# One Hymba layer on one core: the input stages as three queues, stepped behind every contraction tile of the projections

## The chip, the core and the metric

The kernel runs on one core of one Trainium2 chip. The metric is the device time of one execution in microseconds. Three runs of the kernel before took 1739.31 to 1742.88 us, with a median of 1740.18 us. Of the core's engines the text speaks of PE (TensorE, the matmuls), DVE (VectorE), ACT (ScalarE), POOL (GpSimd) and SP (SyncE, which issues the DMAs). Each engine executes its instructions in the order in which the program lists them, and waits where an operand isn't there yet.

## The reference

One layer for 1024 prompt rows and 64 sample rows of width 1024: an adaLN-modulated norm, one input projection whose columns go to 8 RWKV-7 heads and to 8 heads of forgetting attention (FoX), one output projection, and a SwiGLU network. All in fp32.

```python
mod = jax.nn.silu(c) @ w_ada + b_ada
h = _rms_norm(x, norm1_g) * (1 + sc1[:, None]) + sh1[:, None]
proj = h @ w_in
p_rwkv, p_fox = proj[..., :RWKV_COLS], proj[..., RWKV_COLS:]
z = (p_rwkv + (prev - p_rwkv) * shift_mu)            # prev: the row before
r, k, v, dw, da, dg = jnp.split(z, list(RWKV_SPLITS), axis=-1)
decay, a, g = f(tanh(dw) @ w_decay_up), sigmoid(da @ w_aaa_up), sigmoid(dg) @ w_gate_up
...
def step(s, inp):                                    # _rwkv_scan, over the rows
    r_t, w_t, k_t, v_t, kk_t, a_t = inp
    sa = jnp.einsum('bhvk,bhk->bhv', s, -kk_t)
    s = (s * w_t[:, :, None, :] + sa[..., None] * (kk_t * a_t)[:, :, None, :]
         + v_t[..., None] * k_t[:, :, None, :])
    return s, jnp.einsum('bhvk,bhk->bhv', s, r_t)
...
y_fox = _fox_mixer(q, k_all, v_all, lc_all, past)    # softmax(q k + decay bias) v, causal
mix = jnp.concatenate([y_rwkv, y_fox], axis=-1) @ w_out
x = x + gt1[:, None] * mix
ffn = (jax.nn.silu(h2 @ w_ffn_gate) * (h2 @ w_ffn_up)) @ w_ffn_down
```

## The kernel before

The 1088 columns (rows of the reference, laid along the free dimension) are worked in two halves: half 0 has 512 prompt columns, half 1 has 512 prompt and 64 sample columns in two chunks of 288. The normed h of a half lies in SBUF as a high and a low part (`hhi`, `hlo`). `proj` (L298) takes one block of 128 weight columns, splits it in a high and a low part, and multiplies it in `mm3` (L290): three matmuls `pmm` (L294, L295, L296) for each of the 8 tiles of the contraction. They write to a PSUM bank with the tag "mm". PSUM has the further tags "ra", "rb", "ch" and "fx" for the small work. Between the projections stands the small work of the two kinds of heads:

- The RWKV heads go in four pairs j = 0 to 3 per half. `proj_z` computes and shifts the three z of a pair. `rwkv_d` gives decay and a. `rwkv_a` prepares the pair: sums over heads (`pbs`, L375), the products `pA` of each chunk of 64 columns (L464), masked into `At` on DVE (L466), then the triangular systems: `dm` and `mb` through DRAM (L476, L479), 15 steps on DVE with `tb` and `wb` (L488, L490), a transposed copy `mb<-wb` (L491), and the results `dw`, `du` to DRAM (L497).
- `rwkv_b` reads them back as `gt` and `inv` (L513, L514) and merges the 16x16 blocks to 64x64 by small matmuls of 32x32: `pg`, `pw`, `pu`, `pgt` (L523) and `pu` again (L549), each of which needs a copy of the one before. Then come transposes (`pkbt`, `pvt`) and the chain: for each chunk pR (L597), a copy, pSA (L610), a copy, pS (L613), a product on DVE (L617), and pR of the next chunk. Half 0 has 8 chunks for each pair, half 1 has 9.
- `rwkv_n` norms and gates the output y, and writes it to DRAM as `yscr` (L646).
- For FoX, `fox_qk`, `fox_v`, `logf` and `cache_kv` norm, split and store queries, keys, values and the forget sums. `ada_mm` and `ada_fin` (L190, L198) compute the 24 adaLN tiles that later stages need, one with each projection, on a "mm" bank: matmuls with the weights `wada`, a copy `mrow` on ACT, a transpose. `x_stat1` gathers the norm of half 1.

`phase` runs these in the order of a string per half. Capital letters start work, small ones finish it: Z the three z of a pair, D, A, B and N the routines above, Q, K, V the projections of FoX and q, k their norms, C the cache, L `logf`, S `x_stat1`, P early loads of the attention, T and U the last chain of half 0 inside half 1.

```python
ORDER = ("Z0 D0 A0 L B0 D1 Z1 Q0 N0 A1 C0 Z2 q0 D2 V0 O A2 K0 k0 B1 K1 Z3 Q1 q1 V1 N1 D3 A3 V2 C1 S k1 Q2 Q3 B2 q2 N2 K2 k2 V3 K3 k3 C2 C3 q3",
         "T3 Z0 D0 A0 L Z1 K0 D1 U3 B0 A1 D2 Z2 Q0 N0 k0 A2 q0 D3 Q1 B1 K1 q1 Z3 A3 k1 V2 N1 V1 B2 V0 Q2 q2 K3 N2 Q3 q3 P B3 K2 k3 k2 V3")
```

Whole routines stand in the program one after the other. What each engine then executes in which order is settled by a list scheduler at build time: it has the dependences and, as its priority, the place in the program. So a B that stands ahead of a projection is laid between that projection's matmuls as its links come ready. Behind the last projection follow the attention (`psc` scores, `ppt` transposes, `pav` value products), which fills the last pair's chain too, the output projection `po`, and the FFN (`pd` and `pf`), from 778.7 us to the end at 1734.2.

Of the kernel before, what the change touches and what calls it, by code (L numbers as in the profile page):

```python
# [7 lines left out]
F32 = mybir.dt.float32  # L8
# [8 lines left out]
P = 128  # L17
D = 1024
KT = D // P
SP = 1024  # L20
SS = 64
# [13 lines left out]
ORDER = ("Z0 D0 A0 L B0 D1 Z1 Q0 N0 A1 C0 Z2 q0 D2 V0 O A2 K0 k0 B1 K1 Z3 Q1 q1 V1 N1 D3 A3 V2 C1 S k1 Q2 Q3 B2 q2 N2 K2 k2 V3 K3 k3 C2 C3 q3",  # L35
         "T3 Z0 D0 A0 L Z1 K0 D1 U3 B0 A1 D2 Z2 Q0 N0 k0 A2 q0 D3 Q1 B1 K1 q1 Z3 A3 k1 V2 N1 V1 B2 V0 Q2 q2 K3 N2 Q3 q3 P B3 K2 k3 k2 V3")
# [28 lines left out]
class K:  # L65
# [128 lines left out]

    def ada_fin(self, part):
# [36 lines left out]
    def x_stat1(self):  # L232

        nc = self.nc
        acc = self.zpool.tile([P, 576], F32, tag="z", name="xacc")
# [12 lines left out]
        return self.x_rms(Half(1), acc)  # L248

    def x_rms(self, hf, rs):  # L250
        nc, n = self.nc, hf.n
        for off, m in hf.chunks:
            ps = self.ps([P, 512], tag="mm", name="pxs")
# [55 lines left out]

    def proj_z(self, hf, zi):  # L310
# [8 lines left out]
        z = self.zpool.tile([P, 576], F32, tag="z", name="z")  # L319
# [68 lines left out]
    def rwkv_d(self, hf, j, zl):  # L388
# [6 lines left out]
        for off, m in hf.chunks:  # L395
# [8 lines left out]
            for x, (dst, base) in enumerate(((sw, V_W0), (a, V_A0))):  # L404
                nc.vector.tensor_scalar(dst[:, off:off + m], ps[x][:, 0:m], col(base), -43.0, op0=ALU.add, op1=ALU.max)
        self.sigm(sw[:, 0:n], 1.0)
        self.sigm(a[:, 0:n], 1.0)
        cum = self.slot(name="cum", tag="sa")
# [6 lines left out]
        return a, cum  # L415

    def rwkv_a(self, hf, j, z, d):

        nc, vc, O = self.nc, self.vc, self.O
# [4 lines left out]
        zk, zr, zv, sq = z  # L424
        a, ip = d
        pp = self.pp
# [5 lines left out]
            rn[:, off:off + m], ps, 1e-24, None, op0=ALU.max), "ra")  # L432
        nc.scalar.activation(rn[:, 0:n], rn[:, 0:n], AF.Ln, scale=1.0 / 64)
# [4 lines left out]
        kb = self.rpool.tile([P, 9, P], F32, tag="kb", name="kb")  # L438
        nc.vector.tensor_tensor(rk[:, 0:nch, 0:64], ch(kk), pp[:, 0:nch, 0:64], op=ALU.mult)
        nc.vector.tensor_tensor(rk[:, 0:nch, 64:128], ch(zr), pp[:, 0:nch, 1:65], op=ALU.mult)  # L440
        nc.vector.tensor_tensor(kk[:, 0:n], kk[:, 0:n], a[:, 0:n], op=ALU.mult)
        for h in range(2):
            hp = slice(64 * h, 64 * h + 64)
            nc.vector.tensor_tensor(kb[hp, 0:nch, hp], ch(kk)[hp], ch(ip)[hp], op=ALU.mult)
        nc.vector.tensor_scalar(a[:, 0:n], a[:, 0:n], col(V_KA), self.oka[:, j:j + 1], op0=ALU.mult, op1=ALU.add)
        nc.vector.tensor_tensor(zk[:, 0:n], zk[:, 0:n], a[:, 0:n], op=ALU.mult)
        for h in range(2):
            hp, oc = slice(64 * h, 64 * h + 64), slice(64 - 64 * h, 128 - 64 * h)
            nc.vector.tensor_tensor(kb[hp, 0:nch, oc], ch(zk)[hp], ch(ip)[hp], op=ALU.mult)

        nc.vector.scalar_tensor_tensor(zr[:, 0:n], zr[:, 0:n], col(V_RK), zk[:, 0:n], op0=ALU.mult, op1=ALU.mult)
        bon = self.slot(name="bon", tag="bon")
# [1249 lines left out]
```

## Time and profile before

| | |
|---|---|
| median of 3 runs | 1740.18 us (1739.31 to 1742.88) |
| the profiled execution's own time | 1735.94 us, span 1734.2 us |
| mean granted clock of PE | 0.981 |
| first pmm to last pmm (projections and input stages) | 34.8 to 692.3 us |
| from there to the first matmul of the output projection | 692.3 to 778.7 us |
| in the span: PE, DVE, ACT, POOL busy | 1663.8, 1126.6, 729.1, 180.8 us |

In a row of the time line stand start, length (us), engine, line, operation, what is written from what, the shape, and in brackets how long the engine was idle ahead of it and what ended that. In a row of the waits stand engine, operation and line, what was waited for, and the us in total, how often, and the longest. The length of a matmul is modelled and covers that of its neighbours; the rate is read from one start to the next. A wait of an engine that nobody waits for costs nothing.

### The profile page before, as it was taken

The page shows a single profiled execution, that of the slowest core. Times are in us where ns is not written, and L with a number is a line of the kernel's source. Part 1 is how long each engine was busy: PE and PEld are TensorE (multiplying, and loading weights), DVE is VectorE, ACT ScalarE, POOL GpSimd, SP SyncE. Part 2 cuts the span into 40 slices and gives each one's busy share as a digit, 9 for nine tenths or more (in the row PEclk, how much of TensorE's full clock was granted, in tenths as well). Part 3 has the DMA queues.
Part 4 walks back from the last instruction along what each step waited for, and adds up shares of the span by engine and source line. Part 5 has one row for each costly group of instructions (what it writes and reads, how often), then busy time and mean ns, then how long its engine had stood idle before and what let it go on. Part 6 is the DMA issues. An engine that isn't in the chain of part 4 may idle for free.

```text
span 1734.2 us, 33257 instructions
## 1 busy us (share of the span) xinstructions
PE 1663.8 (96%) x12893; PEld 1447.9 (83%) x12893; DVE 1126.6 (65%) x2574; ACT 729.1 (42%) x1532; POOL 180.8 (10%) x412
## 2 busy tenths in 40 slices
PE   5999999999999999889999989999999999999999
PEld 3676766688888888766888889999999999999998
DVE  6676676757686753876877686666666655555545
ACT  4534454553454445765776453333233223211210
POOL 2102121131221212300210000000000000000000
PEclk9999999999899999989999999999999999999999
DMA  8535457632233344566553333222222224433213
GB/s 314 149 95 137 142 140 207 175 93 56 55 76 75 95 121 136 157 194 177 151 177 136 127 115 101 75 75 75 76 75 82 78 87 143 161 98 98 95 37 122
DMA packets 133581, 207.09 MB, mean 119 GB/s; under 512 B 62126, under 2 KB 70350, under 8 KB 133422
## 3 DMA queue, kind: packets, MB, share of 16 engines
q1 hardware_dynamic: 133422, 204.95, 39.3%
q8 instruction: 102, 1.67, 0.4%
q14 instruction: 57, 0.47, 0.1%
HBM read 157.65 MB, written 47.25 MB: 118 GB/s over the span
## 4 chain that ended last, share of the span: by engine, by line
PE 82%; DVE 7%; ACT 7%; DMA 2%; issue 2%; SPq 1%; POOL 0%; DVEq 0%; ACTq 0%; POOLq 0%
PE pd L1264 15%; PE pfc L1153 8%; PE pfe L1153 8%; PE pfa L1153 7%; PE pmm L294 5%; PE pmm L296 5%; PE pmm L295 5%; PE pfb L1153 4%; PE pav L962 2%; PE pbs L375 2%; PE pA L464 2%; PE ppt L940 2%; PE po L294 1%; PE po L295 1%; PE po L296 1%
## 5 line engine op out<-in xcount | busy, mean ns | idle before, releaser
L294 PE MATMUL pmm<-hhi,whi 128*128 128x288 f32 (+1 forms) x624 | 220.7, 354 | 0.7 <-ACT pb L317 0.7
L295 PE MATMUL pmm<-hlo,whi 128*128 128x288 f32 (+1 forms) x624 | 218.2, 350 | 0.0
L296 PE MATMUL pmm<-hhi,wlo 128*128 128x288 f32 (+1 forms) x624 | 218.0, 349 | 0.0
L212 ACT CAST whi<-wraw 128x1024 fp32r<-128x1024 f32 (+2 forms) x116 | 99.3, 856 | 214.4 <-PE pd L1264 167.0
L1264 PE MATMUL pd<-ah,wlo 128*128 128x512 f32 (+1 forms) x528 | 173.5, 329 | 0.0
L1264 PE MATMUL pd<-al,whi 128*128 128x512 f32 (+1 forms) x528 | 173.2, 328 | 0.0
L1264 PE MATMUL pd<-ah,whi 128*128 128x512 f32 (+1 forms) x528 | 173.0, 328 | 0.0
L1268 DVE SCALAR_TENSOR_TENSOR x1t<-pd,mod,x1t 128x512 f32<-128x512 f32 x192 | 91.4, 498 | 110.6 <-PE pd L1264 110.0
L294 PEld LDWEIGHTS pmm<-hhi,whi 128*128 128x128 f32 x624 | 120.3, 193 | 13.5 <-ACT pb L317 2.0
L296 PEld LDWEIGHTS pmm<-hhi,wlo 128*128 128x128 f32 x624 | 120.3, 193 | 10.9 <-issue 1.7
L295 PEld LDWEIGHTS pmm<-hlo,whi 128*128 128x128 f32 x624 | 120.4, 193 | 9.6 <-issue 0.7
L216 DVE TENSOR_TENSOR wlo<-wraw,whi 128x1024 fp32r<-128x1024 f32 (+2 forms) x108 | 103.8, 961 | 26.0 <-ACT whi L212 25.6
L1153 PE MATMUL pfc<-hh,hS 128*128 128x256 f32 (+1 forms) x352 | 102.0, 290 | 4.4 <-ACT hh L1055 4.4
L1264 PEld LDWEIGHTS pd<-al,whi 128*128 128x128 f32 x528 | 99.4, 188 | 7.7
L1264 PEld LDWEIGHTS pd<-ah,whi 128*128 128x128 f32 x528 | 99.3, 188 | 7.7
L1264 PEld LDWEIGHTS pd<-ah,wlo 128*128 128x128 f32 x528 | 99.2, 188 | 7.4
L1153 PE MATMUL pfc<-hl,hS 128*128 128x256 f32 (+1 forms) x352 | 102.3, 290 | 0.0
L1153 PE MATMUL pfc<-hh,lS 128*128 128x256 f32 (+1 forms) x352 | 102.0, 290 | 0.0
L1153 PE MATMUL pfa<-hl,whi 128*128 128x256 f32 (+1 forms) x352 | 101.8, 289 | 0.0
L1153 PE MATMUL pfa<-hh,whi 128*128 128x256 f32 (+1 forms) x352 | 101.7, 289 | 0.0
L1153 PE MATMUL pfa<-hh,wlo 128*128 128x256 f32 (+1 forms) x352 | 101.4, 289 | 0.0
L604 POOL TENSOR_SCALAR sd<-sv,pc 64x64 f32<-64x64 f32 x136 | 72.0, 529 | 172.9 <-DVE sv L617 156.6
(360 smaller groups left out, 4402.0 us busy)
## 6 DMA issues: line engine op xcount, KB each, us to landing
wraw<-in_w_in_dram SPq DMA_DIRECT2D x52, 512.0 KB
wada<-in_w_ada_dram SPq DMA_DIRECT2D x48, 512.0 KB
as<-actscr SPq DMA_DIRECT2D x22, 544.0 KB
wraw<-in_w_gate_dram SPq DMA_DIRECT2D x22, 512.0 KB
wraw<-in_w_up_dram SPq DMA_DIRECT2D x22, 512.0 KB
wraw<-in_w_down_dram SPq DMA_DIRECT2D x40, 256.0 KB
wraw<-in_w_out_dram SPq DMA_DIRECT2D x16, 512.0 KB
actscr<-sg SPq DMA_DIRECT2D x22, 288.0 KB
```

The source lines that it names most:

```text
L212: nc.scalar.copy(hi, src)
L216: eng.tensor_tensor(lo, src, hi.bitcast(F32), op=ALU.subtract)
L294: nc.tensor.matmul(ps[0:M, 0:n], whi[:, k, 0:M], xhi[:, k, off:off + n], start=(k == 0), stop=False)
L295: nc.tensor.matmul(ps[0:M, 0:n], whi[:, k, 0:M], xlo[:, k, off:off + n], start=False, stop=False)
L296: nc.tensor.matmul(ps[0:M, 0:n], wlo[:, k, 0:M], xhi[:, k, off:off + n], start=False, stop=(k == kt - 1))
L375: nc.tensor.matmul(ps[:, 0:n], w, x[:, off:off + n], start=True, stop=True)
L464: nc.tensor.matmul(pa[h][:, i], kb[hp, c + i], rk[hp, c + i], start=True, stop=True)
L604: nc.gpsimd.tensor_scalar(sd[hsl[h]], sv[hsl[h], c, h], pc[hsl[h], c], None, op0=ALU.mult)
L940: nc.tensor.transpose(pt[0:rows, b - b0, t * P:t * P + qn], p[0:qn, pc:pc + rows], self.ident[0:qn, 0:qn])
L1153: nc.tensor.matmul(ps, l[:, k], r[:, s, k], start=(first and k == 0 and y == 0), stop=(k == 3 and y == 2), skip_group_check=True)
L1264: nc.tensor.matmul(ps[:, 0:n], w[:, i], x[:, t:t + n], start=(i == 0 and y == 0), stop=(i == len(fs) - 1 and y == 2))
L1268: nc.vector.scalar_tensor_tensor(dst, ps[:, so - off:so - off + l], self.mod[:, 40 + o, b:b + 1], dst, op0=ALU.mult, op1=ALU.add)
```

## The change

The input stages become generators, small steps that end in a `yield`. Three queues (`Jobs`) hold them: B has the chains and their norms (`rwkv_b`, `rwkv_n`), X the pair preparation (`rwkv_d`, `rwkv_a`, now with the solve, gt, inv, the small blocks and the transposes), F the attention inputs, `logf`, the cache, `x_stat1` and the ada tiles. `proj` has `mm3` written out, and calls `tick` behind each tile of the contraction, so behind every three matmuls. In half 0 a tick takes one step of each queue; in half 1 the ticks go in turns (B and X, B, X and F) while a chain lives, else X and F.

`pause` lets a number of ticks pass: 4 behind the load of mb, 2 ahead of the small blocks, 1 ahead of the norm, each doubled in half 1. `rwkv_a` doesn't begin until the chain of the pair two before has ended. At most 6 z tiles are alive (`room`, `zlive`). `drain` runs a queue to its end where something is needed at once: X ahead of the split of the next half's low-rank inputs, F ahead of the next projection of FoX, F and X at the end of a half, B behind the second half. Weights are loaded two blocks ahead and split one ahead, by a list (`plan`, `raws`, `pre`). Ada tiles, `logf` and the sum of half 1's norm go from "mm" banks to the "fx" bank, the small blocks and the transposes to "ra" banks. The strings have only capital letters left, and most Q, K, V stand behind the Z.

```diff
-ORDER = ("Z0 D0 A0 L B0 D1 Z1 Q0 N0 ...
+ORDER = ("L O D0 Z0 A0 D1 Z1 A1 Q0 C0 C1 D2 Z2 A2 K0 V0 C2 C3 D3 Z3 A3 S Q1 K1 V1 Q2 K2 V2 Q3 K3 V3",
+         "L D0 Z0 A0 D1 Z1 A1 D2 Z2 A2 K0 D3 Z3 A3 Q0 K1 Q1 V0 V1 Q2 P Q3 V2 K2 K3 V3")
+    def ada_job(self, t):
+        part = self.ada_mm(t, None, "fx")
+        yield
+        self.ada_fin(part)
...
+    def tick(self, hf):
+        self.ticks += 1
+        t = self.ticks
+        q = self.jobs
+        if hf.smp:
+            for x in (("BX", "B", "XF")[t % 3] if self.chained or self.st else "XF"):
+                q[x].step()
+        else:
+            for x in "BXF":
+                q[x].step()
+    def pause(self, n):
+        t = self.ticks + n
+        while self.ticks < t and not self.draining:
+            yield
...
     def proj(self, hf, col, evac):
-        if self.pre:
-            whi, wlo = self.pre.pop(0)
-        else:
-            if self.background:
-                self.background.pop(0)()
-            whi, wlo = self.load_w(self.A["w_in"][col // P], [P, KT, P])
-        for off, n in hf.chunks:
+        whi, wlo = self.pre.pop(0)
+        for x, (off, n) in enumerate(hf.chunks):
             ps = self.ps([P, 512], tag="mm", name="pmm")
-            self.mm3(ps, whi, wlo, self.hhi, self.hlo, KT, off, n)
+            for k in range(KT):
+                for y, (w, a) in enumerate(((whi, self.hhi), (whi, self.hlo), (wlo, self.hhi))):
+                    nc = self.nc
+                    nc.tensor.matmul(ps[:, 0:n], w[:, k], a[:, k, off:off + n], start=(k == 0 and y == 0),
+                                     stop=(k == KT - 1 and y == 2))
+                self.tick(hf)
+                if x == 0 and k == 1:
+                    if not self.pre and self.raws:
+                        self.pre.append(self.split_w(self.raws.pop(0), [P, KT, P]))
+                    if len(self.raws) < 2:
+                        self.next_raw()
+                    if self.background:
+                        self.jobs["F"].add(None, self.background.pop(0))
             evac(ps, off, n)
...
         nc.sync.dma_start(mb[0:2 * nb], dm.rearrange("i g x s t -> (i g x) s t"))
+        yield from self.pause(self.lag(hf, 4))
...
             nc.vector.tensor_tensor(wb[0:2 * nb, s + 1:16, 0:s + 1], wb[0:2 * nb, s + 1:16, 0:s + 1], t_, op=ALU.add)
+            if s % 2:
+                yield
...
             elif op == "A":
-                st[j] = self.rwkv_a(hf, j, z.pop(j), d.pop(j))
-            elif op == "B":
-                y[j] = self.rwkv_b(hf, j, st.pop(j))
+                q["X"].add(("A", hf.i, j), self.rwkv_a(hf, j))
+                q["B"].add(None, self.rwkv_b(hf, j))
...
             elif op == "P":
+                self.drain(lambda: (1, 3) in self.solved)
                 self.early()
...
+        self.drain(lambda: not q["F"].q and not q["X"].q)
...
+class Jobs:
+    def __init__(self):
+        self.q, self.done = deque(), set()
+    def add(self, name, gen):
+        self.q.append((name, gen))
+    def step(self):
+        if not self.q:
+            return False
+        name, gen = self.q[0]
+        if next(gen, self) is self:
+            self.q.popleft()
+            self.done.add(name)
+        return True
```

The scheduler still settles the order on each engine. Three places show what it makes of the new program.

The first is on PE, at the last pair of half 1, where its small blocks begin (pmm are the projections' matmuls, fsq a norm of FoX, fv the transposes of a value tile, x9 counts equal rows). Before:

```order
L294 MATMUL pmm<-hhi,whi 128x288
L295 MATMUL pmm<-hlo,whi 128x288
L523 MATMUL pg_8061<-gt,At 32x32
L296 MATMUL pmm<-hhi,wlo 128x288
L294 MATMUL pmm<-hhi,whi 128x288
L523 MATMUL pg_8060<-gt,At 32x32 x18
L375 MATMUL pbs<-fsq,bones 128x288
L295 MATMUL pmm<-hlo,whi 128x288
L523 MATMUL pg_8061<-gt,At 32x32 x17
L523 MATMUL pw_8100<-g_8059,inv_693 32x32 x9
L375 MATMUL pbs<-fsq,bones 128x288
L523 MATMUL pw_8101<-g_8059,inv_693 32x32 x9
```

After, from the last pmm of all:

```order
L356 MATMUL pmm<-hhi,wlo 128x288
L945 MATMUL pkv<-ident,fv 128x128
L428 MATMUL plora<-z,wg 128x288
L945 MATMUL pkv<-ident,fv 128x128 x3
L951 MATMUL pkvs<-ident,fv 64x128
L621 MATMUL pg_7609<-gt,At 32x32 x18
L621 MATMUL pg_7610<-gt,At 32x32
L621 MATMUL pw_7652<-g_7608,inv_693 32x32 x9
L621 MATMUL pg_7610<-gt,At 32x32 x17
L621 MATMUL pw_7653<-g_7608,inv_693 32x32 x9
```

The block has moved from the projections' matmuls, of which 46 followed its first pg before, to a place behind the last of them, with nothing else between its steps.

The second is on SP, at the loads for the first heads of the attention (qsx, k1x, q2x, k2x, vsx) and the last pair's gt and inv. Before:

```order
L868 DMA qsx_8030<-qx 128x512
L870 DMA k1x_8032<-kx 64x512 x2
L873 DMA q2x_8031<-qx 64x512
L874 DMA k2x_8033<-kx 64x512
L591 DMA out_state_p_dram<-state_683 128x64
L873 DMA q2x_8031<-qx 4x512
L874 DMA k2x_8033<-kx 4x512
L879 DMA vsx_8034<-vscr_104 128x512
L514 DMA inv_693<-du_78 32x9x32
L625 DMA out_state_s_dram<-state_683 128x64
L513 DMA gt<-dw_76 32x9x32
L514 DMA inv_693<-du_78 32x9x32
```

After:

```order
L587 DMA gt<-dw_76 32x9x32
L588 DMA inv_693<-du_78 32x9x32
L749 DMA yscr_72<-y 128x576
L1001 DMA qsx_8141<-qx 128x512
L1003 DMA k1x_8143<-kx 64x512 x2
L1006 DMA q2x_8142<-qx 64x512
L1007 DMA k2x_8144<-kx 64x512
L1006 DMA q2x_8142<-qx 4x512
L1007 DMA k2x_8144<-kx 4x512
L1012 DMA vsx_8145<-vscr_103 128x512
```

The loads of both heads have moved from ahead of the last three gt to behind them, and behind the store of the normed y of the pair before.

The third is on DVE, at the second pair of half 1, between the end of its solve (mb<-wb) and the product with pg that follows on it. Before, the first 10 of the 36 rows:

```order
L491 COPY mb<-wb 72x256
L599 COPY R<-pR 64x64
L611 TENSOR_SCALAR sv<-pSA 64x64
L216 TENSOR_TENSOR wlo<-wraw,whi 128x1024
L617 SCALAR_TENSOR_TENSOR state_681<-pS,pc,sd 64x64 x2
L623 COPY y<-pY 64x256
L599 COPY R<-pR 64x64
L431 TENSOR_SCALAR sq<-pbs 128x288 x2
L772 SCALAR_TENSOR_TENSOR fraw<-fraw,vc,fsq 128x576
L611 TENSOR_SCALAR sv<-pSA 64x64
```

After, all of them:

```order
L574 COPY mb<-wb 72x256
L744 SCALAR_TENSOR_TENSOR y<-y,vc,gsq 128x576
L745 SCALAR_TENSOR_TENSOR y<-y,vc,bon 128x576
L747 TENSOR_TENSOR y<-y,plora 128x288
L222 TENSOR_TENSOR wlo<-wraw,whi 128x1024
L747 TENSOR_TENSOR y<-y,plora 128x288
L891 SCALAR_TENSOR_TENSOR fraw<-fraw,qg_150,fsq 128x576
L222 TENSOR_TENSOR fraw<-fraw,shi 128x576
L628 TENSOR_TENSOR g_5969<-pg_5970,qmask 64x288
```

The product with pg has moved from 36 rows behind the solve to 8. The kernel's work is the same before and after: every engine has as many instructions as before, of the same shapes.

More of the change, by code (lines that the diff above doesn't have):

```diff
@@ L1 @@
 import math
+from collections import deque
 from contextlib import ExitStack
@@ new lines, in pause, with room, ztile, drain @@
+    def pause(self, n):
+        t = self.ticks + n
+        while self.ticks < t and not self.draining:
+            yield
+    def room(self, n):
+        while self.zlive + n > 6:
+            yield
+    def ztile(self, name="z"):
+        self.zlive += 1
+        assert self.zlive <= 6
+        return self.zpool.tile([P, 576], F32, tag="z", name=name)
+    def drain(self, cond, queues="BXF"):
+        self.draining = True
+        while not cond():
+            left = [self.jobs[x].step() for x in queues]
+            assert any(left)
+        self.draining = False
@@ L514, in rwkv_b @@
                 nc.sync.dma_start(inv[r, 0:nch, r], du[g, x].rearrange("g s t -> s g t"))
+        kbt = kb
+        sv = self.rpool.tile([P, 9, 2, 64], F32, tag="sv", name="sv")
+        for c in range(0, nch, 4):
+            m = min(4, nch - c)
+            pt = self.ps([P, 4, P], tag="ra", name="pkbt")
+            for i in range(m):
+                nc.tensor.transpose(pt[:, i], kb[:, c + i], self.ident)
+            nc.scalar.copy(kbt[:, c:c + m], pt[:, 0:m])
+            yield
+        for t0 in range(0, nch, 8):
+            m = min(8, nch - t0)
+            pt = self.ps([P, 4, P], tag="ra", name="pvt")
+            for i in range(0, m, 2):
+                w = min(P, (m - i) * 64)
+                nc.tensor.transpose(pt[0:w, i // 2], zv[:, (t0 + i) * 64:(t0 + i) * 64 + w], self.ident)
+            for x in range(min(2, m)):
+                for h in range(2):
+                    nc.scalar.copy(sv[64 - 64 * h:128 - 64 * h, t0 + x:t0 + m:2, h],
+                                   pt[64 * x:64 * x + 64, 0:(m - x + 1) // 2, 64 * h:64 * h + 64])
+            yield
+        self.zlive -= 1
+        yield from self.pause(self.lag(hf, 2))
         def small(name, blocks, mm):
[L518 removed]
+            pg = [self.ps([P, 9, 32], tag=t, name=name) for t in ("ra", "ra")]
             for c in range(nch):
@@ L646, in rwkv_n @@
         nc.sync.dma_start(self.yscr[hf.i][:, j], y[:, 0:n])
+        if j == 3:
+            self.zlive -= 1
+        self.ended.add(4 * hf.i + j)
+        self.chained = False
     def ones_rows(self):
@@ L1274, in down, with phase @@
             acts = new
-    def phase(self, hf, order, late):
+    def phase(self, hf, order):
         nc = self.nc
+        q = self.jobs
         with self.tc.issue_after(self.last.ins):
```

206 lines of the change are left out of this document (126 added, 80 removed).

## The prediction

> **What bounds the kernel now.** I read the page first, then the busy time by windows cut at the stages, then the waits of PE and the time lines of single stretches.
>
> ```profile
> span 1734.2 us, 33257 instructions
> ...
> PE 1663.8 (96%) x12893; PEld 1447.9 (83%) x12893; DVE 1126.6 (65%) x2574; ACT 729.1 (42%) x1532; POOL 180.8 (10%) x412
> ...
> PE 82%; DVE 7%; ACT 7%; DMA 2%; issue 2%; SPq 1%; POOL 0%; DVEq 0%; ACTq 0%; POOLq 0%
> ...
> L294 PE MATMUL pmm<-hhi,whi 128*128 128x288 f32 (+1 forms) x624 | 220.7, 354 | 0.7 <-ACT pb L317 0.7
> ```
>
> PE is the bound as a whole (96% busy, 82% of the chain that ended last). The contraction matmuls of the projections, pmm, hardly wait: 0.7 us before 624 of them. So neither weights nor evacuations hold the projections up, and a better prefetch of weights is worth nothing here. The windows cut the span at the first projection (34.8), the end of half 0 (about 330), the last pmm (692.3) and the first matmul of the output projection (778.7); the last rows are one block of small matmuls and the dense FFN.
>
> ```profile
> 34.80:330.00 295.20, 284.96 (x2245) 204.54 (x2245) 205.24 (x544) 139.41 (x288) 51.32 (x120) 0.97 0.52 148
> 330.00:692.30 362.30, 352.44 (x3319) 299.98 (x3318) 236.91 (x641) 173.33 (x411) 78.65 (x161) 0.98 0.34 92
> 692.30:778.70 86.40, 74.17 (x430) 55.96 (x428) 69.35 (x213) 60.68 (x177) 17.05 (x55) 0.94 0.62 178
> 674.80:683.80 9.00, 9.00 (x266) 7.29 (x265) 2.39 (x6) 6.17 (x15) 4.44 (x6) 1.00 0.84 249
> 1200.00:1735.00 535.00, 530.88 (x3718) 507.79 (x3716) 298.66 (x563) 127.22 (x214) 0.00 (x0) 1.00 0.29 94
> ```
>
> The columns are length, then busy time (and instructions) of PE, PEld, DVE, ACT, POOL, then granted clock, DMA share, GB/s. In the two halves PE is idle 10.2 and 9.9 us, 20.1 together; in the 86.4 us behind them, where the last chain and the attention run, 12.2 us. The granted clock of 0.97 and 0.98 costs something too: a mean of 0.97 is half speed in 6% of 295.2 us, which loses half of that, 8.9 us; 0.98 loses 7.2 us. Everything that a reordering of this stage can win is therefore some 20 us of idle time, 16 us of clock, and what hides inside busy rows.
>
> ```profile
> PE pbs L375 <- ACT fsq L759: 2.9, 3, 1.4
> PE pS L613 <- ACT sv L612: 2.2, 5, 0.8
> PE plf L680 <- ACT fl L676: 1.9, 2, 1.5
> PE pu L549 <- ACT gt L545: 1.7, 2, 1.5
> ...
> PE pg L523 <- DVE y L644: 1.1, 1, 1.1
> PE plora L399 <- DVE sw L405: 1.0, 1, 1.0
> ```
>
> These are the largest waits of PE from 34.8 to 692.3: many small ones, no large one. What the changed order does to links like these decides the time.
>
> ```profile
> 301.73 0.40 PE L296 MATMUL pmm<-hhi,wlo 128*128 128x512 f32 x1
> 301.96 0.39 PE L294 MATMUL pmm<-hhi,whi 128*128 128x512 f32 x1
> 302.21 0.46 PE L597 MATMUL pR<-sv,At 128*128 128x128 f32 x2
> ...
> 303.22 0.43 PE L610 MATMUL pSA<-R,inv 128*128 128x64 f32 x2
> ...
> 304.34 0.49 PE L613 MATMUL pS<-sv,kb 128*128 128x128 f32 x2
> ...
> 305.61 0.46 PE L597 MATMUL pR<-sv,At 128*128 128x128 f32 x2
> ```
>
> This is one chunk of a chain in before: 3.4 us from pR to pR, three links of about 1 us, with pmm at 0.23 us apart (301.73 to 301.96) laid into them. Before has this cover already.
>
> **The change, part by part.** *Instructions.* Every engine has the same instructions in both orders, PE 10988. Work costs 0; only waits, clock and overlap can differ. PE goes from small work to pmm runs and back about as often (321 runs of pmm before, 307 after), so I cost the switching at 0, too: 14 switches at about 0.1 us (pR follows its pmm by 0.25 us in the rows above, a pmm by 0.23) bound it at -1.4 us.
>
> *Chains (queue B).* Each link needs 0.7 to 1.1 us of other PE work behind it. Laying the trace's spacings (0.23 us a pmm of 512 columns as above, 0.13 to 0.14 one of 288, as in the last rows below) under both orders, the missing cover of all links comes to 20.4 us before (4.0 in half 0, 12.5 in half 1, 3.9 behind the last pmm) and 21.0 after (6.2, 8.4, 6.4). Fewer links are short after (71 for 104), but more are bare. Value 0; bounds -5 and +5, the difference of the parts taken one-sided.
>
> *The last pair's block.* After, all 180 small matmuls of the last pair stand behind the last pmm, back to back, and so do its links pg, pw, pu, pgt, pu, pR. In before 9.0 us (674.8 to 683.8) hold the block with four pbs and some pmm between the links, PE 9.00 busy.
>
> ```profile
> 675.48 0.76 PE L523 MATMUL pg<-gt,At 32*32 32x32 f32 x36
> 676.17 0.75 PE L375 MATMUL pbs<-fsq,bones 128*128 128x288 f32 x2
> ...
> 683.10 0.75 PE L549 MATMUL pu<-inv,gt 32*32 32x32 f32 x18
> ```
>
> The matmul time only changes its place: what goes behind the last pmm left the phase ahead of it. The lost cover is what counts: five links. Bare, each takes between nothing (half of a block still runs while the first half is copied) and the 1.5 us that the pu row of the waits shows; at about 0.8 us, the nearest chain link (longest wait for sv 0.8), five are **+4 us**, bounds 0 and 7.5. As cover is gone, the chain of that pair, which began at 689.7, 2.6 us ahead of the last pmm, begins some 7 us behind it.
>
> *Solve path (queue X).* Pair preparation is followed by copies through DRAM, the 15 steps of the triangular solve on DVE, and back through DRAM to gt, on which pg waits. The rows show its shortest passage in before, pair 4:
>
> ```profile
> 420.20 0.49 PE L464 MATMUL pA<-rk,kb 64*128 64x128 f32 x2
> ```
> ```profile
> 426.77 0.32 SPq L479 DMA_DIRECT2D mb<-dm  x1
> ...
> 447.17 0.46 SPq L514 DMA_DIRECT2D inv<-du  x1
> ```
> ```profile
> 430.56 0.17 DVE L488 TENSOR_TENSOR tb<-mb,wb 72x15 f32<-72x15 f32 x1 [1.98 <-DMA mb<-dm]
> ...
> 440.35 0.37 DVE L491 COPY mb<-wb 72x256 f32<-72x256 f32 x1
> ```
> ```profile
> 451.06 0.24 PE L523 MATMUL pg<-gt,At 32*32 32x32 f32 x2
> ```
>
> From the last pA to pg 30.4 us. After, the matmuls between the two add up to 25 to 27 us of spacings for five pairs, 32 to 38 for three; the phase runs 1.22 times longer than such a sum (657.5 us for 537 us of spacings), so 31 to 33 us for the five. DVE has to be counted for the same stretch: with the trace's durations over the new order, it must pass for the third pair of half 0 7.4 us of work before the solve, 16.6 during it and then the way from 440.7 to 451.1, 10.4 us: 34.4 against 32 us. For the fourth it is 9.8, 21.2 and 10.4 against 39. Both come out 2.4 us late, the others even. In before 36 to 61 us of spacings lay there in seven of eight pairs. Value **+5**; bounds 0 and, if every one of the five tight pairs waits 5 us, +25. Queued behind a waiting pg are the projections themselves (PE is in order), and DVE's first product with pg, with all evacuations behind it.
>
> *Attention inputs (queue F).* Steps of norm, logf and ada follow their producers sooner: nine of the 24 ada transposes have only two pmm (0.46 us) behind their copy, and pbs comes 0.4 to 1.7 us behind the square, where before mostly lay more than 3.
>
> ```profile
> 31.23 0.33 PE L198 MATMUL pada<-ident,mrow 128*128 128x128 f32 x1 [0.59 <-ACT mrow L193]
> ```
>
> Bare, the transpose waits 0.59 us; nine with a fifth to a third of it left make +1 to +2, and the norms, which waited 2.9 us in all, perhaps +1 more. Against that logf's wait (1.9) is laid between tiles, and the waits on sw and y (1.0, 1.1) have more matmuls ahead: -4. Together **-1.5**, bounds -6 and +6.
>
> *SP.* The loads for attention heads 0 and 1 now stand behind the last gt and behind the normed y of the pair before. In before they went out from 644.8 on, long ahead of the scores at 692:
>
> ```profile
> 644.81 0.58 SPq L868 DMA_DIRECT2D qsx<-qx  x1
> ```
>
> After, at 0.6 us an issue, the first score matmul has its operands only some 4 us after that y. The bare block of 7 us covers it: 0, or +4 without it.
>
> The sum is +4 +5 -1.5 = +7.5 us on the profiled execution's 1735.94 (its span of 1734.2 and 1.74 around it): 1743.4. That execution is 4.2 us below the median of the runs, 1740.18, so the comparable time is 1747.7, and I say **1747**.
>
> A cross-check by the tail's own rows:
>
> ```profile
> 689.70 0.46 PE L597 MATMUL pR<-sv,At 128*128 128x128 f32 x2
> ...
> 692.07 0.30 PE L295 MATMUL pmm<-hlo,whi 128*128 128x288 f32 x1
> 692.21 0.30 PE L296 MATMUL pmm<-hhi,wlo 128*128 128x288 f32 x1
> ```
> ```profile
> 728.50 0.65 PE L375 MATMUL pbs<-y,bmean 128*128 128x288 f32 x2
> ```
>
> The last chain takes 38.8 us (689.7 to 728.5), then 50.2 us to 778.7. After, from the last pmm: 1.5 us of rest, 7 of block, a chain of 34 to 38.8 (28 instead of 36 value products lie in it, so it may be shorter), 50.2 to 52: 93 to 99 for 86.4, +7 to +13. About 6 us of this left the stretch ahead (its spacings sum to 532 us for 537): +1 to +7. It agrees with the +4.
>
> **Rivals.** *Denser stage (faster).* One small step per three matmuls feeds DVE and ACT evenly, and the "mm" banks are free of ada and logf; idle falls. For it: PEld is 204.54 of 295.20 (69%) and 299.98 of 362.30 (83%) in the halves, against 507.79 of 535 (95%) in the FFN, so busy rows hide slack. If half of the 20.1 us idle and half of the 16.1 us of clock go, that is -18: **1722**; all of both less the block's 4, -32. Against it: link cover by order is equal, and small matmuls load weights for less time than they take. The Trainium skill, "Perfetto Trace Analysis", section on identifying the most-contended engine, says that matmul busy time is a poor measure of how full TensorE is, and asks for the share of weight loads; by it the halves have 14 to 26% of headroom, which is the case for this rival. The FFN row agrees that a full stretch shows 95%.
>
> *A new wait (slower).* pg reaches gt too early. Price: 5 us in each of five pairs, 25 us, decided by whether a solve takes longer than the 31 to 33 us that the matmuls now leave. Stretches of waiting or small matmuls then also lower the clock: after, 14.8 us of spacings in half 0 lie without a pmm, where before's longest was 7.4 there and 8.7 in half 1. Half speed in such a stretch costs 7 us. With both at two thirds, +21: **1761**; both in full give +32. The Trainium skill, "TensorE: Matmul & The Clock Gate", Part 1 on the clock gate, states that the array drops to half clock after an idle window of about 3.4 us. The halves' mean of 0.97 and 0.98, with no single wait over 1.5 us in the rows above, shows that here the clock falls without so long a wait, so the rule by itself would let this change off.
>
> *No effect.* The scheduler sorts the new program into much the same order: **1740**. Against it: the block's place and SP's queue have plainly moved.
>
> **How the numbers follow.** My forecast's case (waits moved, small loss) 0.42: of it 0.30 slower, 0.09 same, 0.03 faster. Denser stage 0.33, faster. New wait 0.17, slower. No effect 0.08. That is faster 0.36, same 0.17, slower 0.47, with 0.2% (3.5 us, about what a measurement can tell here) as the bound. The likeliest case alone spans 1739 to 1755. For the range I go down to -24 (between the denser stage's -18 and its full -32) and up to +30 (just short of its rival's full price): 1716 to 1770.
>
> **What the profile after would show.** Idle of PE between first and last pmm: near 20 us if I am right, near 10 for the denser stage, over 35 for the new wait. The tail from last pmm to first output projection: 93 to 99 us. A row "pg from DMA gt" in the waits of PE is the solve path; its absence refutes my +5. Link waits in the last block, pu on gt or inv above all, should sum to about 4. A granted clock below 0.97 in half 0 tells of the bare stretch. I would be wrong if DVE, at 70% in half 0 (205.24 of 295.20), were what paces the pmm through waits inside busy rows: then even feeding wins more than the idle rows show.

## The result, and the profile after

The change is slower. Four runs took 1764.29 to 1766.54 us, median 1766.53; before took 1741.53 us beside them. The ratio is 1.0138, with a 95% interval of 1.0118 to 1.0159. The profiled execution took 1764.29 us, its span 1762.6, so 28.4 us more span than before's 1734.2.

The windows are cut at the same events as in the prediction: first pmm, end of half 0, last pmm, first and last matmul of the output projection, end. The columns are those explained there. After:

```profile
34.90:348.40 313.50, 288.27 (x2259) 205.03 (x2260) 208.81 (x545) 150.00 (x308) 52.51 (x119) 0.96 0.49 144
349.10:698.20 349.10, 335.13 (x3040) 291.31 (x3039) 231.45 (x632) 161.35 (x382) 78.77 (x157) 0.97 0.30 82
698.20:801.90 103.70, 84.21 (x690) 65.15 (x689) 72.15 (x220) 62.94 (x186) 20.14 (x60) 0.90 0.55 165
801.90:1014.50 212.60, 201.19 (x1232) 170.17 (x1231) 157.30 (x293) 128.66 (x258) 25.31 (x40) 0.97 0.52 156
1014.50:1762.60 748.10, 737.53 (x5405) 710.56 (x5403) 436.58 (x826) 210.84 (x366) 0.00 (x0) 0.99 0.28 94
```

The same windows of before, the two that the prediction did not show:

```profile
778.70:987.60 208.90, 199.51 (x1232) 168.78 (x1231) 157.60 (x293) 129.00 (x257) 25.41 (x40) 0.98 0.53 155
987.60:1734.20 746.60, 735.55 (x5405) 709.06 (x5403) 436.68 (x826) 210.70 (x366) 0.00 (x0) 1.00 0.29 94
```

| stretch | before, us | after, us | idle of PE before | idle of PE after | clock before | clock after |
|---|---|---|---|---|---|---|
| half 0 | 295.2 | 313.5 | 10.2 | 25.2 | 0.97 | 0.96 |
| half 1 | 362.3 | 349.1 | 9.9 | 14.0 | 0.98 | 0.97 |
| last pmm to output projection | 86.4 | 103.7 | 12.2 | 19.5 | 0.94 | 0.90 |
| output projection | 208.9 | 212.6 | 9.4 | 11.4 | 0.98 | 0.97 |
| FFN | 746.6 | 748.1 | 11.1 | 10.6 | 1.00 | 0.99 |

PE's busy time over these windows is the same, 1646.6 and 1646.3 us. By that account what was added is idle time (28 us over all rows), most of it in half 0 and behind the last pmm. The clock fell too: counted as in the prediction (1 less the mean clock, times the span), half speed lost 33 us before (0.981 of 1734.2) and 49 us after (0.972 of 1762.6). The 16 us of clock and the 28 us of idle together are more than the 28.4 us that the span grew, so the rows don't divide the loss between them. Half 1 is shorter because 279 matmul records left it (3040 for 3319); 260 more stand behind the last pmm (690 for 430). The waits of PE from 34 to 800 us show no single culprit, and hardly one row that waits for a DMA:

```profile
PE pbs L435 <- DVE z L527: 10.3, 3, 9.5
PE pS L707 <- ACT sv L705: 6.8, 9, 1.3
PE pR L689 <- DVE sv L711: 5.6, 6, 2.7
PE pw L621 <- DVE g L628: 4.4, 4, 1.9
...
PE pSA L703 <- ACT R L692: 2.4, 6, 0.6
...
PE pg L621 <- DMA gt<-dw: 0.6, 1, 0.6
```

One stands out: 9.5 us in the preparation of the first pair, at 74 us. The matmul that waits there is the next on PE behind a sum; no pmm stands between, and the low part of the next weights was split only at 89.36 us:

```profile
73.11 0.39 PE L356 MATMUL pmm<-hhi,wlo 128*128 128x512 f32 x1
73.33 1.02 PE L435 MATMUL pbs<-sq,bones 128*128 128x512 f32 x2
83.83 2.08 PE L435 MATMUL pbs<-z,bones 128*128 128x512 f32 x2 [9.48 <-DVE z L527]
```

A quieter thing turned out to weigh more. In before, the decay of pair 1 (the DVE row a<-plora) is done long before the small blocks of pair 0, which begin with pg:

```profile
94.42 0.75 DVE L405 TENSOR_SCALAR a<-plora,vc 128x512 f32<-128x512 f32 x1 [0.37 <-PE plora L402]
```
```profile
130.47 0.24 PE L523 MATMUL pg<-gt,At 32*32 32x32 f32 x2
...
182.72 0.69 PE L523 MATMUL pg<-gt,At 32*32 32x32 f32 x32
```

After, pair 0's pg comes at the same time, but pair 1's decay only behind it, and pair 1's pg 23 us later than before:

```profile
146.48 0.74 DVE L465 TENSOR_SCALAR a<-plora,vc 128x512 f32<-128x512 f32 x1
```
```profile
130.40 0.24 PE L621 MATMUL pg<-gt,At 32*32 32x32 f32 x2
...
206.06 0.24 PE L621 MATMUL pg<-gt,At 32*32 32x32 f32 x2
...
624.77 0.24 PE L621 MATMUL pg<-gt,At 32*32 32x32 f32 x2
...
701.16 0.76 PE L621 MATMUL pg<-gt,At 32*32 32x32 f32 x38
```

Queue X takes one generator after the other: decay, preparation, the way through DRAM, the solve, the way back, the small blocks, and only then the next pair's decay. A pair takes it about 75 us (130.40 to 206.06, and 624.77 to 701.16 for the last). Before's later pairs follow one another no faster (72.7 to 78.0 us from pg to pg in half 1); only its first two are 52.3 us apart. So the 23 us lost at pair 1 are never made up: every later pg is 21 to 28 us behind its place in before, and the last pair's block begins at 701.16, where before had its first pg at 674.85. By then the pmm are used up (last at 698.2), so the block is bare:

```profile
699.82 0.44 PE L945 MATMUL pkv<-ident,fv 128*128 128x128 f32 x2 [0.59 <-ACT fv L906]
700.93 0.30 PE L951 MATMUL pkvs<-ident,fv 128*64 128x128 f32 x1 [0.68 <-ACT tok L947]
701.16 0.76 PE L621 MATMUL pg<-gt,At 32*32 32x32 f32 x38
703.33 1.01 PE L621 MATMUL pw<-g,inv 32*32 32x32 f32 x15 [1.41 <-DVE g L628]
...
705.82 1.01 PE L621 MATMUL pw<-g,inv 32*32 32x32 f32 x15 [0.55 <-DVE g L628]
...
709.21 1.75 PE L621 MATMUL pgt<-gt,At 32*32 32x32 f32 x36 [0.66 <-ACT inv L640]
711.35 1.58 PE L651 MATMUL pu<-inv,gt 32*32 32x32 f32 x36 [0.39 <-ACT gt L646]
712.86 0.80 PE L689 MATMUL pR<-sv,At 128*128 128x128 f32 x2
713.31 0.77 PE L1043 MATMUL psc<-k1x,qsx 128*128 128x256 f32 x2
...
751.61 0.65 PE L435 MATMUL pbs<-y,bmean 128*128 128x288 f32 x2
```

From pg to the chain's first pR it takes 11.7 us, 3.0 of them waits on links; 36 small matmuls take 0.76 us in before (675.48), and 38 as much at the block's start here, but 36 take 1.58 and 1.75 us at its end. The chain itself (712.86 to 751.61, 38.75 us) and what follows are as long as before, and the chain begins 14.7 us behind the last pmm, where it began 2.6 us ahead of it. This difference equals the 17.3 us that the stretch behind the last pmm grew, but it doesn't explain them: in a run below the chain begins as late, and the stretch is far shorter. By the windows, 10.0 of the 17.3 us are busy time of PE, for the block's matmuls now stand here and run at a lower clock, and 7.3 us are idle. The attention's first scores (psc) moved, too: 15.1 us behind the last pmm (713.31), where before had them 0.3 us behind it (692.48).

### The profile page after: what moved, and what is told of

Its sections match the earlier page's. It is cut to its first block, busy times and chain, and to the rows that moved or that the text cites. A ratio compares the mean times of both kernels' runs of the same rounds, so it can differ in the third digit from the quotient of the medians.

```text
span 1762.6 us, 33280 instructions
## 1 busy us (share of the span) xinstructions
PE 1665.4 (94%) x12893; PEld 1452.8 (82%) x12893; DVE 1127.8 (64%) x2574; ACT 730.6 (41%) x1532; POOL 185.1 (11%) x412
## 4 chain that ended last, share of the span: by engine, by line
PE 76%; DVE 9%; ACT 6%; DMA 4%; issue 4%; POOL 1%; SPq 0%; DVEq 0%; ACTq 0%; POOLq 0%
PE pd L1397 15%; PE pmm L356 12%; PE pfc L1286 7%; PE pfe L1286 7%; PE pfa L1286 7%; PE pfb L1286 4%; PE pav L1095 2%; PE pbs L435 2%; PE ppt L1073 2%; PE pA L543 1%; PE po L306 1%; PE po L304 1%; PE po L305 1%; PE pS L707 1%; PE pR L689 1%
```

## The experiments

Each ratio is against before in runs on the same chip; before took 1741.0 to 1743.3 us in them.

**Two single edits, both together, and one in the kernel before.** The weights of pair 1 were loaded at 63.44 us, behind the output of `logf` on SP, so the first suspicion for the 9.5 us fell on `logf`.

```diff
-ORDER = ("L O D0 Z0 A0 D1 Z1 A1 Q0 ...
+ORDER = ("O D0 Z0 A0 D1 Z1 A1 L Q0 ...
```

> The change with logf moved in half 0's string from its head to behind A1, nothing else. Theory of the late weights: the load of the weights for pair 1 went out at 63.4 us because it stood on SP behind logf's output, so their split came late and PE stood bare for pair 0's preparation (9.5 and 0.6 us of waits, and matmuls at half speed). Then the 9.5 us wait is gone and the time falls by 10 to 14 us, to 1753 to 1757 us. Rival, the loss is spread over many small waits: the wait moves elsewhere, and the time stays at 1764 to 1769 us.

Measured: 1764.10 us, 1.0119 (1.0083 to 1.0155). The wait is still there, 9.47 us, and the time is in the range of the rival. The theory of `logf` and SP fell.

The next edit takes `rwkv_d` out of queue X, into a queue of its own that waits only until the pair before is past the use of the shared tiles:

```diff
     def rwkv_d(self, hf, j, zl):
+        while 4 * hf.i + j - 1 not in self.prepped:
+            yield
...
-        while 4 * hf.i + j - 2 not in self.ended:
+        while 4 * hf.i + j - 2 not in self.ended or j not in self.d:
...
         self.zlive -= 2
+        self.prepped.add(4 * hf.i + j)
         yield
...
-            for x in (("BX", "B", "XF")[t % 3] if self.chained or self.st else "XF"):
+            for x in (("BX", "BD", "XF")[t % 3] if self.chained or self.st else "XDF"):
...
-            for x in "BXF":
+            for x in "BXDF":
```

> The change with rwkv_d in a fourth queue of its own, so that the decay of the next pair no longer waits for the solve and the small blocks of the pair before. logf stays where it was. Theory of the serial queue X: the last pair's small blocks stand behind the last pmm because X takes 75 us for each pair, one after the other; here they come ahead of the last 54 pmm, the block is covered, and the tail from the last pmm to the output projection falls from 103.7 to about 88 us: time down by 8 to 17 us, to 1750 to 1758 us, with pair 0's stall still there. Rival, the block's place costs nothing because the same matmuls only change places: 1764 to 1769 us.

Measured: 1754.99 us, 1.0075 (1.0053 to 1.0098). The time is in the range of the theory. The last pair's pg comes at 683 us, ahead of the last pmm at 701, and the stretch behind the last pmm falls from 103.7 to 95.8 us, not to the 88 that I expected. (The profiled execution took 1761.17 us, the longest of the seven.)

> The change with both edits, late logf and the queue for rwkv_d. If both theories hold, the gains add: 18 to 31 us off, 1736 to 1748 us. If one stall only hides the other, no more than the larger one: 1750 to 1757 us.

Measured: 1750.35 us, 1.0048 (1.0032 to 1.0065). Against the change's median that is 16.2 us, where the two edits alone gave 2.4 and 11.5. They add up or a little more, short of the 18 us that I asked for, and the time lies in the range of the rival; since late `logf` left the stall where it was, this run doesn't test whether the two stalls add.

The last of the four is the kernel before with its last block put behind the pmm:

```diff
-... Q3 q3 P B3 K2 k3 k2 V3")
+... Q3 q3 P K2 k3 k2 V3 B3")
```

> The kernel before with one token of half 1's string moved: B3 (small blocks and chain of the last pair) behind V3, so that its block stands behind the last pmm as in the change. Theory of the bare block: links without cover and the half clock cost 8 to 17 us, 1750 to 1758 us. Rival, the place costs nothing: 1738 to 1745 us, as before.

Measured: 1740.89 us, 0.9993 (0.997 to 1.0016): no cost at all. Its windows (half 0, half 1, and last pmm to output projection) show why:

```profile
35.70:332.70 297.00, 286.06 (x2240) 204.96 (x2241) 204.63 (x542) 139.01 (x287) 51.24 (x120) 0.97 0.51 146
333.00:685.40 352.40, 343.23 (x3049) 292.72 (x3047) 234.93 (x635) 167.21 (x392) 76.02 (x156) 0.98 0.33 91
685.40:777.50 92.10, 79.69 (x685) 62.41 (x685) 72.48 (x214) 63.03 (x189) 19.82 (x60) 0.93 0.58 168
```

Half 1 is 9.9 us shorter, the stretch behind it 5.7 us longer, and idle behind the last pmm is 12.4 us, as before. The block stands behind the last pmm here too, yet scores of the attention fill it:

```profile
688.71 0.73 PE L523 MATMUL pu<-inv,g 32*32 32x32 f32 x35
689.37 0.38 PE L910 MATMUL psc<-k1x,qsx 128*128 128x256 f32 x1
689.59 0.28 PE L912 MATMUL psc<-k2x,q2x 68*128 68x256 f32 x1
...
691.03 0.38 PE L910 MATMUL psc<-k1x,qsx 128*128 128x256 f32 x1
...
701.54 0.46 PE L597 MATMUL pR<-sv,At 128*128 128x128 f32 x2
```

The chain begins at 701.54, 16.3 us behind the last pmm and so later than the change's, and yet the stretch is 11.6 us shorter than the change's. So in the kernel before, neither the block's place nor the chain's late start costs anything by itself. The operands of these scores were loaded from 647 us on; in the change the loads go out from 701.62 us on, behind the last gt and the store of y. That these late loads keep other work out of the change's block, and that this is the price, is argued and not shown. In the run with the own queue for `rwkv_d` the loads had gone out by 692, and still the first score came 12.9 us behind the last pmm:

```profile
683.07 0.43 SPq L1004 DMA_DIRECT2D qsx<-qx  x1
...
691.83 0.34 SPq L1015 DMA_DIRECT2D vsx<-vscr  x1
```
```profile
713.84 0.56 PE L1046 MATMUL psc<-k1x,qsx 128*128 128x256 f32 x1
```

**Late ada tiles.** The stall of the first pair again: here the 24 ada tiles are started only after 64 ticks.

```diff
-                    if self.background:
+                    if self.background and self.ticks > 64:
```

> The change with the ada tiles of the projections started only after 64 ticks (behind pair 0's projections and preparation), nothing else; all 24 still run. The late-logf run left the 9.5 us wait of pair 0's preparation where it was, so the logf theory has fallen. New theory: the ada tiles' loads of 512 KB stand between the weights' loads in the first projections, and the scheduler, which counts on weights that late, lays pair 0's preparation bare ahead of the next weight's split; with the ada tiles later, 42 pmm stand inside the preparation. Then the 9.5 us wait goes and the time falls by 8 to 13 us from the change's 1766.5: 1753 to 1759 us. Rival: the preparation's waits only move, 1763 to 1769 us.

Measured: 1770.65 us, 1.0166 (1.0135 to 1.0197). The time is above both of my ranges. The wait is gone (0.4 us where 9.5 stood, and a new one of 2.9 us for a `whi`), idle in half 0 falls by 7.1 us, and the time doesn't fall. In the profiled execution half 0 is as long as in the change, at a clock of 0.93 instead of 0.96:

```profile
36.70:350.30 313.60, 295.50 (x2162) 212.18 (x2162) 207.81 (x542) 148.73 (x303) 53.40 (x118) 0.93 0.46 134
```

So taking out the largest wait of the profile brought nothing by itself. With the queue for `rwkv_d` it is different:

> Late ada tiles, the own queue for rwkv_d and late logf together. If the stall of pair 0 and the serial queue X are the two causes of the loss, their gains add to e4's 1750.4: 8 to 13 us less, 1737 to 1743 us, level with before (1741). If something else in the steps costs too (chains paced by ticks), it stays above before: 1744 to 1750 us.

Measured: 1747.76 us, 1.0026 (1.0009 to 1.0043). Half 0 is now 291.0 us, shorter than before's 295. The time is in the second range: something else costs, too.

> The same with logf at the head of half 0's string again, as in the change. Late logf gave 2 to 5 us by itself; if that was only the ring of weight buffers (logf's weights and the ada tiles share it), it gives nothing once the ada tiles are late, and this run equals the one with late logf within 2 us; else it is 2 to 5 us slower.

Measured: 1755.68 us, 1.0077 (1.0053 to 1.0101), 7.9 us above the run with late `logf`, more than either theory had. `logf` at the head costs more than the ring of weight buffers explains; which part of it costs that is open.

**The block filled.** Is it the small matmuls that bring the half clock?

```diff
+        def fill(f):
+            if hf.smp and j == 3:
+                for k in range(6):
+                    nc.tensor.matmul(f[:, 288:512], self.hhi[:, 0, 0:P], self.hhi[:, k, 0:224], start=True, stop=True,
+                                     skip_group_check=True)
```

> The change with 30 more matmuls of 224 columns in the last pair's small blocks, six behind each of the five steps, into an unused part of the same PSUM bank; nobody reads them (3 to 4 us of added work). In the change this block takes 11.7 us, stands behind the last pmm, and is followed by 20.5 us of half clock (from 702.1). Theory of the clock: it is the stretch of small matmuls and waits without dense ones that brings the half clock; filled, the clock loss of the tail falls from 10.2 to under 5 us, and the time by 2 to 6 us in spite of the added work, to 1760 to 1765 us. Rival: only the links' waits (3.0 us) are filled, the half clock stays, and the time is level or up to 3 us longer, 1766 to 1770 us.

Measured: 1766.17 us, 1.0155 (1.0129 to 1.018), level with the change, as the rival had it. (The profiled execution took 1757.79 us, the shortest of the five.) Idle behind the last pmm falls from 19.5 to 10.9 us, but the half clock stays. In the change and in this run:

```profile
702.10:722.60 20.50, 16.99 (x249) 14.69 (x250) 6.47 (x22) 5.61 (x20) 4.01 (x7) 0.50 0.53 168
```
```profile
702.30:726.20 23.90, 22.75 (x274) 19.72 (x275) 6.39 (x26) 4.96 (x17) 4.36 (x9) 0.50 0.50 149
```

The half clock began at 702.1, only 1 us into the block, and 30 matmuls of 224 columns laid into the block didn't end it. What came ahead of it, in the change, was a stretch mostly between the last pmm and the block in which PE was busy for 1.94 of 3.41 us (first row; the second is the step behind it):

```profile
698.71:702.12 3.41, 1.94 (x44) 1.10 (x42) 1.90 (x5) 1.90 (x4) 2.44 (x2) 1.00 0.47 78
702.12:705.53 3.41, 1.94 (x52) 1.81 (x52) 1.67 (x6) 0.00 (x0) 0.00 (x0) 0.50 0.90 283
```

My theory of the clock fell; idle was exchanged for added work, and the chain began at 715.2 us, not earlier than in the change (712.9).

**Back to the level of before, and each edit taken out again.** `logf` is moved in half 1, too (behind A1, and K0 behind A3):

```diff
-         "L D0 Z0 A0 D1 Z1 A1 D2 Z2 A2 K0 D3 Z3 A3 Q0 ...
+         "D0 Z0 A0 D1 Z1 A1 L D2 Z2 A2 D3 Z3 A3 K0 Q0 ...
```

> Late ada tiles, own queue for rwkv_d, late logf in half 0 and now in half 1 too (behind A1, and K0 behind A3). By the order the last pair's block then has 65 pmm behind it (54 in the version before it), and the pairs of half 1 come 6 to 48 pmm earlier. Theory that the place of the pair preparation in the stage sets the tail: the tail falls from 93.7 to about 88 us, the time from 1747.8 to 1741 to 1746, level with before. Rival: the tail is set by the last chain and the attention alone: 1745 to 1750.

Measured: 1742.70 us, 1.0005 (0.9989 to 1.0021): in the range of the theory and level with before, with ticks, pauses and all else of the change in place. Behind the last pmm it takes 89.0 us. The decay of the last pair now comes ahead of the block of the pair before:

```profile
559.52 0.51 DVE L467 TENSOR_SCALAR a<-plora,vc 128x288 f32<-128x288 f32 x1
```
```profile
597.74 0.24 PE L624 MATMUL pg<-gt,At 32*32 32x32 f32 x2
...
666.44 0.24 PE L624 MATMUL pg<-gt,At 32*32 32x32 f32 x2
```

> The run that came level with before (late ada tiles, own queue for rwkv_d, late logf in both halves), with rwkv_d put back into queue X. Theory: the serial queue X is the largest part of the loss, and late loads alone can't mend it: 1753 to 1763 us. Rival: with the loads mended X is no longer late, since the last block has 21 pmm behind it here: 1743 to 1748.

Measured: 1761.29 us, 1.0124 (1.0101 to 1.0147). With `rwkv_d` back in queue X, 18.6 us of the gain are lost, as the theory had it, and the stretch behind the last pmm is 103.1 us again. Half 0 and that stretch, first of this run and then of the level run:

```profile
35.90:337.30 301.40, 285.13 (x2161) 204.72 (x2162) 207.35 (x541) 148.47 (x303) 55.16 (x118) 0.97 0.49 140
691.30:794.40 103.10, 84.36 (x650) 62.92 (x649) 71.62 (x218) 62.12 (x185) 19.72 (x60) 0.93 0.54 163
```
```profile
36.70:326.90 290.20, 281.78 (x2161) 199.78 (x2161) 209.59 (x550) 147.96 (x301) 60.78 (x120) 0.99 0.50 142
689.50:778.50 89.00, 72.96 (x409) 54.18 (x408) 69.20 (x208) 58.71 (x173) 14.14 (x50) 0.94 0.57 169
```

So 11.2 us of the gain stand in half 0 and 14.1 behind the last pmm, and half 1 gives 8.3 back (362.3 us for 354.0). The serial queue costs from the first half on, not only at the end.

> The same level run with the ada tiles started with the first projection again, so that pair 0's preparation is bare once more (no pmm between its first and second pbs in the order). Theory: that stall costs what its wait says, 8 to 13 us: 1751 to 1756 us. Rival, from the run with late ada tiles alone, where 7 us less idle in half 0 brought no time: it is made up behind, 1743 to 1748 us.

Measured: 1745.76 us, 1.002 (1.0007 to 1.0033). The bare wait of pair 0 is back, 9.45 us, and costs 3.1 us, which the intervals don't tell from nothing; the time is in the range of the rival. Half 0 is 15 us longer and half 1 12 us shorter (305.7 and 350.5 for 290.2 and 362.3), with 153 more matmul records in half 0 and 150 fewer in half 1: small work that went on while the pmm stood still was missing later.

> The level run with queue X stepped on every tick of half 1 while a chain lives (two of three for D and F swapped in turn as before). By the order the last block then has 127 pmm behind it instead of 65. If the tail is still set by when the last chain starts, the tail falls from 88.9 to under 84 us and the time to 1736 to 1740, below both kernels; if a covered block is all that counts, it stays at 1741 to 1745.

Measured: 1755.90 us, 1.0081 (1.0061 to 1.0101). The tail falls further than expected, from 89.0 to 61.6 us, and the time rises by 13. From half 1 to the end of the output projection PE is idle 49.0 us where the level run was idle 38.9, and half 1 takes 392.0 us for 362.3, at a clock of 0.93 for 0.96, with a stretch of 30.7 us at half clock:

```profile
666.00:696.70 30.70, 24.88 (x117) 19.89 (x116) 8.50 (x31) 7.63 (x24) 8.40 (x17) 0.50 0.36 118
```

So an earlier last chain isn't better without end; both of my theories missed this. No version was faster than the kernel before.

The edit of queue X tells best, since it was made four times over different versions (medians, us). Each time the two intervals are apart. The first and the last row compare runs that had other runs of before beside them; by their ratios to before the differences are 11.0 and 20.7 us.

| the rest of the version | rwkv_d in X | rwkv_d in its own queue | difference |
|---|---|---|---|
| the change | 1766.5 | 1755.0 | -11.5 |
| and late logf in half 0 | 1764.1 | 1750.4 | -13.7 |
| late ada tiles | 1770.7 | 1755.7 | -15.0 |
| late ada tiles, late logf in both halves | 1761.3 | 1742.7 | -18.6 |

Late `logf` in half 0 gave 2.4, 4.6 and 7.9 us (the first within its interval), late `logf` in half 1 5.1, late ada tiles -4.1, -0.7, 2.6 and 3.1. Of these only the 7.9 us is clear of the intervals. Half 0's `logf` was not put back into the level version.

## Why the prediction was right or wrong

The direction and the range held: slower, and 1766.5 lies in 1716 to 1770. The size of the likeliest case did not: 1747 was +6.8 us against the median of before, and it was +25, outside that case's own 1739 to 1755. That the direction held is partly luck: of the +7.5, +5 stood for a wait that didn't come. The upper end of the range came from the price of a rival's wait, which didn't come either. By my own marks (idle from first to last pmm over 35 us) the profile after, with 39 us, is that of the rival with a new wait, but not with the wait that I named.

- *Instructions at 0*: held. Both pages have 12893 matmul records, and PE's busy time agrees within 1 us in the sum of the windows.
- *Chains at 0, bounds -5 to +5*: too low. Waits on the chain's links (pS, pR, pSA) are 6.8, 5.6 and 2.4 us from 34 to 800. Before had 3.1 for pS, the rest under 1 each. That is about 10 us more. The sums of missing cover came out equal (20.4 and 21.0 us), though the prediction saw that fewer links would be short and more of them bare. Why the sum missed the 10 us is open.
- *The last pair's block, +4, bounds 0 to 7.5*: the waits on its links were sized well (3.0 us). By the order the block has 126 matmuls (252 records in the trace), not 180; no term hung on that. I took its matmuls at full clock, 7 us; it took 11.7 in all, and the chain began 14.7 us behind the last pmm where I had 7. The stretch took 103.7 us against my 93 to 99.
- *SP, 0 or +4*: here my reading may have been the wrong way about. I let the block cover the late loads of the attention. The kernel before with its late block shows that the attention can cover such a block, at no cost at all. That the loads behind gt take this cover away, and what that costs, no run tests by itself.
- *Solve path, +5*: the passage was sized well, from the end of pA to pg 25 to 41 us, and 31.2 for the last pair. But hardly anything waited: pg waited 0.6 us for gt in all. The scheduler put pg where gt had come. The step that failed lies one further: I asked what the solve's end meets on PE, and not what queues behind the solve in X. The next pair's decay and preparation do, 75 us a pair, and four pairs of runs put 11 to 19 us on that by their medians. I had the fact in the diff (rwkv_d and rwkv_a in one queue) and in the order, and costed only the wait that it might add.
- *Attention inputs, -1.5*: the waits that I wanted gone are gone, and no wait of an ada transpose above 0.9 us in all came in. But a wait of 9.5 us came in at the first pair, which I had not seen. It went with late ada tiles and stayed with late `logf`; alone it costs little.
- *Clock*: I had it only in the rival. The mean of 0.981 fell to 0.972, 16 us more of lost clock. The Trainium skill, "TensorE: Matmul & The Clock Gate", Part 1 on the clock gate, gives an idle window of about 3.4 us as what brings half clock. Ahead of 702.1 the rows show waits of 0.59 and 0.68 us, none near that, so in this case the half clock came without so long a wait. PE was busy 1.94 of the 3.41 us ahead of it; the last section counts such stretches in all traces.

The rival of the denser stage failed: evenly laid steps filled no slack. The reading of weight loads as headroom found none that this order could use. (From its own 69, 83 and 95% it is 12 to 26%, not 14 to 26.)

## What to carry to other kernels

Where steps are put in queues, work out the length of a queue's cycle for each item, and ask what stands behind it in that queue, not only what waits for its result. Such a delay can show far from where it arises: here 23 us were lost at pair 1, and the last pair's block, 26 us late, fell behind the last of the work that had covered it. The length of the largest wait of a profile isn't its price. Here it was 9.5 us, and taking it out changed the time by -4.1 to 3.1 us; take such a wait out before building on it.

## What the runs showed of the hardware that was not expected

In these traces the granted clock is full or half and changes in steps of 3.41 us. Counted in such steps over the 14 kept traces, a step at full clock in which PE was busy for less than 1.5 us was followed by half clock 43 times of 43, one with 1.5 to 2.4 us 90 times of 227, and one with more 41 times of 6446. Out of half clock, none of 49 steps with PE busy for less than 2.4 us led back to full clock, and 174 of 325 busier ones did. So half clock came without one long wait, too, where several short ones fell in a step. This is a count, not an experiment, and it leaves open what decides among the busier steps. With 30 matmuls of 224 columns laid into the block, PE was busy 22.75 of 23.9 us, and the clock stayed at 0.50. In the run with the faster queue X it stayed there for 30.7 us with PE busy 24.88. The profiled execution of f1 (late ada tiles alone) lost a wait of 9.5 us and was no faster, at a clock of 0.93 in half 0 for 0.96.
